# Reading and multiplying the second gate's weights after the output projection instead of beside it

## The chip, the cores and the metric

The kernel runs on one core of a Trainium2 chip. The metric is the time of one execution on the device in microseconds (us); the median of several runs is compared. Times inside a run are counted from the first instruction of the profiled execution.

## What is computed

One decoder layer on 256 tokens of width 2048, all in float32. A conditioning vector `c` gives six vectors of 2048 numbers (shift, scale and gate for each of two sub-layers):

```
mod = SiLU(c) @ W_ada + b_ada            # W_ada is 2048 x 12288: six blocks of 16 MiB
h = x * (1 + scale1) + shift1
y = W_out [ GatedDeltaNet(h) || ForgettingAttention(h) ]
x = LayerNorm(alpha * x + (1 + gate1) * y)
h = x * (1 + scale2) + shift2
y = MoE(h)      # router: best of 4 groups, in it the best 2 of 8 SwiGLU experts
x = LayerNorm(alpha * x + (1 + gate2) * y)
```

The change is about `gate2`, the sixth block of `W_ada`. Nothing needs it before the last residual: it becomes the row `g2` from the tenth pair of experts on.

## The kernel before, in words

**The stages.** The mixer with its input projections runs to about 580 us. The output projection (`w_out`, lines 899 to 944; its matmuls are recorded at L916) runs from 580 to 710 us, the first layer norm and the router (lines 946 to 1045) to 725 us, and 32 experts in 16 pairs from there to 1670 us. Each expert reads three 4 MiB matrices (`wg`, `wu`, `wd`) in tiles of 1 MiB, whatever tokens it gets. All these reads are issued from SP, in one queue.

**The gate as it was.** `ada_full(s)` (L274) is a generator that handles one block of `W_ada`: for each of 16 `j` it asks for a tile `waf` and reads 1 MiB into it (L283). Then either TensorE multiplies it, four matmuls 32 columns wide into the PSUM tile `paf` (L289; float32 matmuls stand twice in the trace), or VectorE adds it, scaled, to a sum `S` (L232, L234; two instructions a tile), as the table `DVEJ` says. At the end the sum `S` is folded into `paf` (L295), copied to `asum` (L297) and turned into a column by small matmuls (`pac`, L300). `ada_step(n)` runs n such steps. In the output projection, 6, 6 and 4 steps stand behind its first three quarters (`WREST`), 8 tiles for TensorE and 8 for VectorE.

**The output projection.** It runs over four quarters `n` of 512 columns. Each quarter reads four tiles `w_out` (L906), splits every 128 rows on ScalarE (`wh`, L373) and VectorE (`wl`, L374), multiplies 6 times for each of 16 `kt` (`pwo`, L916), then applies gate 1 (L933, L934), transposes the result (`put`, L937), and adds its part of the router's logits (`plg`, L942).

**The buffers.** `wtile` gives one of 6 tiles of 1 MiB, the ring W, used by `w_out`, by `waf` and later by experts' weights. `etile` deals the experts' tiles out over the ring E (5 tiles), then W (6), then E2 (1), and again. The three first tiles of expert 0 are pages. So expert 0 takes three pages and the five E tiles; expert 1 takes the six W tiles, E2, and the first E tile again, once expert 0 has used it. PSUM has two tiles of two banks (`bank2`: `pwo`, later `pye` and `pcb`), two single banks `d` (`dbank`), one `a` (`abank`) and one `m`. `ebank` gives `a` at every third request, but only when no block of `W_ada` is left.

**Order.** Each engine works in order. A planner at build time puts each engine's instructions, and SP's reads, into an order by its own cost estimates, following the program's order where several are ready. The matmuls of the experts' part (`pe_matmul`, recorded at L1051) are told to keep the program's order.

**Experts.** `load_gu(e)` (L1079) asks for the eight tiles of `wg` and `wu`, `stage_a` gathers the tokens (`pga`) and multiplies (`pgu`), `load_d` (L1090) asks for the `wd` tiles of both experts of a pair, and `stage_b` multiplies them (`pye`).

Of the kernel before, what the change touches and what calls it, by code (L numbers as in the profile page):

```python
# [6 lines left out]
F32 = mybir.dt.float32  # L7
# [8 lines left out]
S = 256  # L16
# [20 lines left out]
RORD = (3, 4, 2, 5)  # L37
OVP = 8
CEN = (1,)
WREST = (6, 6, 4, 0)  # L40
DVEJ = {3: 10, 4: 10, 2: 10, 5: 8}
DVET = {(0, 0): 0, (0, 1): 0, (4, 0): 2, (4, 1): 2, (8, 0): 5, (8, 1): 5}
CONVP = dict.fromkeys(('q0', 'k0', 'v0', 'q1', 'k1', 'v1'), (1, 2))
CONVN = {'v0': 0, 'v1': 1}
# [4 lines left out]
def build(tc, A, out, dbg=None, stop=None):  # L49
# [15 lines left out]
    with ctx:  # L65
# [9 lines left out]
        turn_ = [0]  # L75

        def page(name, dt=F32):
            return pg.tile([128, 2048], dt, name=name, tag="P")
# [7 lines left out]
        def dbank(name, dt=F32):  # L86
            return pd.tile([128, 512], dt, name=name, tag="d")

        def abank(name):
            return pa.tile([128, 512], F32, name=name, tag="a")  # L90

        def ebank(name):

            turn_[0] += 1
            return abank(name) if turn_[0] % 3 == 0 and not ada_units else dbank(name)

        def bank2(name):
            return pacc.tile([128, 1024], F32, name=name, tag="acc")
# [6 lines left out]
        fp = front.enter_context(tc.tile_pool(name="fp", bufs=2))  # L105
# [167 lines left out]

        def ada_full(s):  # L274

            ps = abank("paf")
            vj = spread(DVEJ[s], 16)
            S_ = None
            if vj:
                S_ = page("S5") if s == RORD[-1] else fp.tile([128, 2048], F32, name="S", bufs=1)  # L280
            for j in range(16):
                w = wtile("waf")
                SP.dma_start(w[:, :2048], wada_v[:, j, s * D:(s + 1) * D])  # L283
                c = cs[:, j:j + 1]
                if j in vj:
                    mac(S_, w[:, :2048], c, 2048, j == vj[0])
                else:
                    for g in range(4):
                        PE.matmul(ps[32 * g:32 * g + 32, :], c.to_broadcast([128, 32]), w[:, g * 512:(g + 1) * 512],  # L289
                                  start=j == 0, stop=j == 15 and not vj)  # L290
                if j < 15:
                    yield
            if vj:
                for g in range(4):
                    PE.matmul(ps[32 * g:32 * g + 32, :], ones[:, 0:32], S_[:, g * 512:(g + 1) * 512], start=False, stop=True)  # L295
            a = wk.tile([128, 512], F32, name="asum", bufs=1)
            V.tensor_copy(a, ps)  # L297
            pc = dbank("pac")
            for i in range(4):
                PE.matmul(pc[:, i * 4:i * 4 + 4], a[:, i * 128:(i + 1) * 128], sel4, start=i == 0, stop=i == 3, skip_group_check=True)  # L300
            dst = gcol[s] if s in gcol else mod2n[:, s - 3]
            V.tensor_tensor(dst.rearrange("p (h i) -> p h i", h=4), pc[:, 0:16].rearrange("p (i h) -> p h i", h=4),
                            bc[:, s].rearrange("p (h i) -> p h i", h=4), op=OP.add)
            if s in (3, 4):
                pp = dbank("pap")
                av = a.rearrange("p (q j) -> p j q", j=16)
                for j in range(16):
                    for h in range(4):
                        PE.matmul(pp[32 * h:32 * h + 32, j * 4:j * 4 + 4], av[:, j, :], sel4, start=j == 0, stop=j == 15, skip_group_check=True)
                for h in range(4):  # L310
                    b = slice(32 * h, 32 * h + 32)
                    V.tensor_tensor(mod2[b, s - 3], pp[b, 0:64].rearrange("p (j h) -> p j h", h=4)[:, :, h], bcp[b, s - 3], op=OP.add)
            yield
# [3 lines left out]
        ada_left = [0]  # L317
# [15 lines left out]
        for dt2 in range(8):  # L333
            ps = dbank("pxt")
# [566 lines left out]
        for n in range(4):  # L901
            ns = slice(n * 512, (n + 1) * 512)
            ws = []
            for q in range(4):
                w = wtile("w_out")
                SP.dma_start(w[:, :2048].rearrange("p (k n) -> p k n", k=4),  # L906
                             w_out[q * 512:(q + 1) * 512, ns].rearrange("(k p) n -> p k n", p=128))
                ws.append(w[:, :2048].rearrange("p (k n) -> p k n", k=4))
            ps = bank2("pwo")

            def terms(kt, part_, wx, first, en):
                for t in range(2):
                    ts = slice(t * 128, (t + 1) * 128)
                    o_ = [oT[kt // 4][:, a, kt % 4, ts] for a in range(2)]
                    for i, h_ in enumerate(o_[:1] if part_ else o_):
                        PE.matmul(ps[:, t * 512:(t + 1) * 512], h_, wx[:, :512], start=first and i == 0, stop=en, skip_group_check=True)  # L916

            g1 = ut[:, 512:1024]
            ACT.activation(g1, bc_row(gcol[2], n, ebank("pg1"), ut[:, 1024:1536]), AF.Copy)
            late = []  # L920
            for kt in range(16):
                wh, wl = split1(ws[kt // 4][:, kt % 4, :], 512)
                terms(kt, 0, wh, kt == 0, False)
                late.append((kt, wl))
                if len(late) > LATE:
                    terms(late[0][0], 1, late[0][1], False, False)
                    late.pop(0)
            for i, (kt, wl) in enumerate(late):
                terms(kt, 1, wl, False, i == len(late) - 1)
            ada_step(WREST[n])  # L930
            for t in range(2):
                pt_ = ps[:, t * 512:(t + 1) * 512]
                V.tensor_tensor(pt_, pt_, g1, op=OP.mult)  # L933
                V.scalar_tensor_tensor(u[t][:, ns], u[t][:, ns], ALPHA, pt_, op0=OP.mult, op1=OP.add)  # L934
                px_ = ebank("put")
                for i in range(4):
                    PE.transpose(px_[:, i * 128:(i + 1) * 128], u[t][:, n * 512 + i * 128:n * 512 + (i + 1) * 128], ident)  # L937
                ui = ut[:, t * 1536:t * 1536 + 512]
                ACT.activation(ui, px_, AF.Copy)
                V.bn_stats(st[:, t, n, :], u[t][:, ns])  # L940
                for i in range(4):
                    PE.matmul(plg[:, t * 36:(t + 1) * 36], ui[:, i * 128:(i + 1) * 128], wr[:, n * 4 + i, :], start=n + t + i == 0,  # L942
                              stop=n * 4 + i == 15, skip_group_check=True)
# [64 lines left out]
        M = sm("M", 2, 4, 8)  # L1008
        V.tensor_tensor(M, og[:, :, :, None].to_broadcast([128, 2, 4, 8]), p12[:, :, None, :].to_broadcast([128, 2, 4, 8]), op=OP.mult)
        Mf = M.rearrange("p t g e -> p (t g e)")  # L1010
        prk = abank("prk")
        PE.matmul(prk[:, 0:64], Us, Mf, start=True, stop=False, skip_group_check=True)
        PE.matmul(prk[:, 32:64], ones, Mf[:, 0:32], start=False, stop=False, skip_group_check=True)
        for t in range(2):
# [237 lines left out]
        def overflow():  # L1252
# [14 lines left out]
            with tc.If(full > CAP):  # L1267
                GP.iota(idx, pattern=[[1, NE]], base=0, channel_multiplier=0, allow_small_or_imprecise_dtypes=True)
                V.memset(ec, 0.0)
                with tc.For_i(0, NE, 1) as e:  # L1270
# [8 lines left out]
                    for b in range(2):  # L1279
# [30 lines left out]
                        for t in range(2):  # L1310
                            for n in range(4):
                                combine_q(t, n, ye, woT, pb[n % 2])

        sp_, xg = slots_of(0)
        weighted(0, sp_)
        how = None
        pieces = []
        for p in range(NE // 2):
            more = p + 1 < NE // 2
            if p:  # L1320
                fill = {j: [f] for j, f in zip(CJ, pieces)}
            else:
                fill = {4 * q: [lambda q=q: gathered(q, sp_, xg)] for q in range(4)}
            gu0 = stage_a(load_gu(2 * p), xg, 0, fill)
            if not p:
                how = weights_of(0, sp_)
            hid = []
            fill = {TJ: [lambda: hid.append(hidden(gu0, 0, sp_))]}
            if ROWS <= p < ROWS + len(ROW):
                for n in range(4):  # L1330
                    fill.setdefault(RJ[n], []).append(lambda n=n: row_part(p - ROWS, n))
            if not more:
                xr = residual()
            w1 = load_gu(2 * p + 1)
            wd = []
            if p == OVP:
                wd = load_d(p, range(2))
                overflow()
            gu1 = stage_a(w1, xg, 1, fill)
            if more:  # L1340
                nsp, nxg = slots_of(p + 1)
                weighted(p + 1, nsp)
                for q in range(2):
                    gathered(q, nsp, nxg)
            hid.append(hidden(gu1, 1, sp_))
            if not more:
                gated(xr)
            else:
                for q in range(2, 4):
                    gathered(q, nsp, nxg)  # L1350
                nhow = weights_of(p + 1, nsp)
                wd += load_d(p, range(len(wd), 4))
                pieces = combine(p, stage_b(wd, hid), how)
                sp_, xg, how = nsp, nxg, nhow
# [63 lines left out]
```

## Time and profile before

| | us |
|---|---|
| median of 3 runs | 1711.81 (1706.97 to 1716.03) |
| profiled execution, its own time | 1716.68 |
| its span, first to last instruction | 1714.9 |
| PE (matmul) busy | 1612.3 (94%) |
| DVE busy | 795.8 (46%) |
| ACT busy | 390.5 (23%) |
| read from memory | 583.77 MB |

How to read it: a busy TensorE is not one at its peak, since its matmuls are pipelined and overlap in the records. The profile also gives the share of time in which the 16 DMA engines moved data, and how fast; this has to be read stage by stage.

### The profile page before, as it was taken

The numbers are of one execution on the slowest core, as the hardware profiler recorded it, in microseconds if no ns is written. First come the engines' busy times: TensorE is split into PE (matmuls) and PEld (weight loads), VectorE is DVE, ScalarE is ACT, GpSimd is POOL, SyncE is SP. The second block draws the span as 40 slices with busy tenths as digits, with TensorE's granted clock in tenths as the row PEclk, the third lists the DMA queues.
The fourth block names the chain that finished last, engine by engine and source line by source line (L and its number), as shares of the span: only waits on it lengthen the run. The fifth ranks groups of instructions, "written<-read, shape, count | busy, mean of one in ns | idle before, by whom it ended". The sixth has DMA issues, their size and how long they took to land. (4 is left out here: it accounts for less than half of the span.)

```text
span 1714.9 us, 23756 instructions
## 1 busy us (share of the span) xinstructions
PE 1612.3 (94%) x9709; PEld 952.6 (56%) x9709; DVE 795.8 (46%) x1538; ACT 390.5 (23%) x699; POOL 64.8 (4%) x80
## 2 busy tenths in 40 slices
PE   5999899999999999799999999999899999999984
PEld 2777777789778866643444344344444434434431
DVE  3568889768747777522322222132222212213166
ACT  1443355344324533400000000000000010010101
POOL 3000001000000000000000000000000000000001
PEclk8899899999999999899999999999999999999997
DMA  9989877527747879869999999999899999999994
GB/s 289 314 296 340 306 263 272 173 99 259 265 152 285 343 276 344 337 260 403 426 424 425 425 425 424 424 425 425 356 425 424 403 424 384 424 394 402 407 412 151
DMA packets 122193, 587.47 MB, mean 343 GB/s; under 512 B 9600, under 2 KB 11824, under 8 KB 65248
## 3 DMA queue, kind: packets, MB, share of 16 engines
q1 hardware_dynamic: 121328, 585.35, 86.4%
q8 instruction: 78, 1.28, 0.3%
q0 software_dynamic: 752, 0.56, 0.3%
q14 instruction: 35, 0.29, 0.0%
HBM read 583.77 MB, written 2.10 MB: 342 GB/s over the span
## 5 line engine op out<-in xcount | busy, mean ns | idle before, releaser
L1051 PE MATMUL pgu<-wu,xg 128*64 128x512 f32 x1024 | 467.5, 598 | 22.6 <-DMA wu<-in_w_up 20.8
L1051 PE MATMUL pgu<-wg,xg 128*64 128x512 f32 x1024 | 465.0, 597 | 2.0 <-DVE xg L1123 2.0
L1051 PEld LDWEIGHTS pgu<-wg,xg 128*64 128x64 f32 x1024 | 131.2, 136 | 197.3 <-issue 188.0
L1051 PE MATMUL pye<-wd,sp 128*64 128x512 f32 x960 | 215.7, 595 | 0.0
L1123 DVE TENSOR_SCALAR xg<-pga,aff 128x128 f32<-128x128 f32 x256 | 87.5, 405 | 264.4 <-PE pga L1051 264.4
L1051 PEld LDWEIGHTS pgu<-wu,xg 128*64 128x64 f32 x1024 | 129.9, 136 | 105.5 <-issue 59.9
L391 PE MATMUL pi<-hH,wh 128*128 128x256 f32 x640 | 168.1, 294 | 3.0 <-ACT wh L373 1.8
L391 PE MATMUL pi<-hL,wh 128*128 128x256 f32 x640 | 165.8, 290 | 0.0
L1051 PEld LDWEIGHTS pye<-wd,sp 128*64 128x64 f32 x960 | 68.0, 137 | 135.8 <-issue 135.5
L391 PEld LDWEIGHTS pi<-hH,wh 128*128 128x128 f32 x640 | 124.4, 194 | 18.4 <-issue 12.8
L1051 PEld LDWEIGHTS pga<-sp,xn 128*128 128x128 f32 x1024 | 118.7, 194 | 15.8 <-issue 14.6
L1161 ACT ACTIVATE gu<-pgu 128x512 f32<-128x512 f32 x32 | 19.1, 597 | 475.8 <-PE pgu L1051 475.8
L1201 DVE SCALAR_TENSOR_TENSOR yy<-pye,wc,yy 128x1024 fp32r<-128x1024 f32 x30 | 38.4, 1281 | 190.5 <-ACT yy L1200 190.1
L391 PEld LDWEIGHTS pi<-hL,wh 128*128 128x128 f32 x640 | 124.3, 194 | 1.1 <-DVE hL L354 0.2
L1051 PE MATMUL pga<-sp,xn 128*128 128x128 f32 x1024 | 123.4, 279 | 1.1 <-DVE tot L1034 1.1
L1212 DVE TENSOR_TENSOR acc<-pcb,acc 128x1024 f32<-128x1024 f32 x56 | 68.5, 1224 | 117.1 <-PE pcb L1051 117.1
L391 PE MATMUL pi<-hH,wl 128*128 128x256 f32 x640 | 105.4, 290 | 3.1 <-DVE wl L374 3.1
L391 PEld LDWEIGHTS pi<-hH,wl 128*128 128x128 f32 x640 | 89.3, 195 | 5.3 <-DVE wl L374 4.6
L1200 ACT ACTIVATE yy<-pye,wc 128x1024 fp32r<-128x1024 f32 x30 | 33.4, 1115 | 255.6 <-PE pye L1051 255.6
L234 DVE SCALAR_TENSOR_TENSOR S<-waf,cs,S 128x1024 f32<-128x1024 f32 x68 | 90.5, 1343 | 0.0
L916 PE MATMUL pwo<-wh,oT 128*128 128x512 f32 x256 | 73.4, 405 | 0.3 <-ACT wh L373 0.3
L1051 PE MATMUL pcb<-yy,ohT 128*128 128x512 f32 x240 | 71.8, 420 | 1.8 <-DVE acc L1212 1.8
(410 smaller groups left out, 1925.2 us busy)
## 6 DMA issues: line engine op xcount, KB each, us to landing
wu<-in_w_up SPq DMA_DIRECT2D x128, 1024.0 KB, 18.7
wg<-in_w_gate SPq DMA_DIRECT2D x128, 1024.0 KB, 17.4
wd<-in_w_down SPq DMA_DIRECT2D x126, 1024.0 KB, 18.3
waf<-in_w_ada SPq DMA_DIRECT2D x64, 1024.0 KB, 5.1
wah<-in_w_ada SPq DMA_DIRECT2D x32, 1024.0 KB, 7.3
w_out<-in_w_out SPq DMA_DIRECT2D x16, 1024.0 KB, 6.7
w_q<-in_w_in SPq DMA_DIRECT2D x8, 1024.0 KB, 7.0
w_k<-in_w_in SPq DMA_DIRECT2D x8, 1024.0 KB, 5.6
```

What stands on the lines that cost most here:

```text
L234: V.scalar_tensor_tensor(S_[:, hs], w[:, hs], c, S_[:, hs], op0=OP.mult, op1=OP.add)
L391: PE.matmul(ps[:, m * 256:(m + 1) * 256], wx[:, m * 128:(m + 1) * 128], h_, start=first and m % 2 == 0 and i == 0, stop=en, skip_group_che ...
L916: PE.matmul(ps[:, t * 512:(t + 1) * 512], h_, wx[:, :512], start=first and i == 0, stop=en, skip_group_check=True)
L1051: return tc.keep_in_program_order(PE.matmul(*a, **k))
L1123: V.tensor_scalar(xg[:, j * 128:(j + 1) * 128], ps[:, i * 128:(i + 1) * 128], aff[:, 0, j:j + 1], aff[:, 1, j:j + 1], op0=OP.mult, op1=OP.add)
L1161: ACT.activation(gu, ps, AF.Copy)
L1200: ACT.activation(y[:, 0], ps[h], AF.Copy, scale=how[0])
L1201: V.scalar_tensor_tensor(y[:, 1], ps[h], how[0], y[:, 0].bitcast(F32), op0=OP.mult, op1=OP.subtract)
L1212: V.tensor_tensor(acc[t][:, hs], pc, acc[t][:, hs], op=OP.add)
```

## The change

Gate 2 has no VectorE tiles any more (`DVEJ` is 0 for block 5), and all its 16 steps stand in one place: behind the router in the program, after a `load_gu(0)` that has moved ahead of them. Its PSUM tile comes from `bank2`, its page `S5` is gone, `ebank` may give bank `a` between two blocks, and the router's rank matmuls (`prk`) take a `dbank`.

```
-WREST = (6, 6, 4, 0)
-DVEJ = {3: 10, 4: 10, 2: 10, 5: 8}
+DVEJ = {3: 10, 4: 10, 2: 10, 5: 0}
...
-            return abank(name) if turn_[0] % 3 == 0 and not ada_units else dbank(name)
+            return abank(name) if turn_[0] % 3 == 0 and (not ada_units or ada_left[0] == 0) else dbank(name)
...
-            ps = abank("paf")
+            ps = bank2("paf")[:, :512] if s == RORD[-1] else abank("paf")
...
-                S_ = page("S5") if s == RORD[-1] else fp.tile([128, 2048], F32, name="S", bufs=1)
+                S_ = fp.tile([128, 2048], F32, name="S", bufs=1)
...
-            ada_step(WREST[n])
...
-        prk = abank("prk")
+        prk = dbank("prk")
...
+        w00 = load_gu(0)
+        ada_step(16)
         sp_, xg = slots_of(0)
...
-            gu0 = stage_a(load_gu(2 * p), xg, 0, fill)
+            gu0 = stage_a(load_gu(2 * p) if p else w00, xg, 0, fill)
```

## Rows read from the trace of the kernel before

**Rows 1.** The page, part 2: busy tenths and GB/s in 40 slices of 42.9 us.
```profile
PE   5999899999999999799999999999899999999984
...
DMA  9989877527747879869999999999899999999994
GB/s 289 314 296 340 306 263 272 173 99 259 265 152 285 343 276 344 337 260 403 426 424 425 425 425 424 424 425 425 356 425 424 403 424 384 424 394 402 407 412 151
```

**Rows 2.** Windows: length; busy of PE, PEld, DVE, ACT, POOL; clock, DMA, GB/s.
```profile
580.00:709.70 129.70, 125.87 (x622) 94.06 (x614) 86.74 (x132) 51.55 (x97) 7.57 (x6) 0.99 0.89 341
...
709.00:725.00 16.00, 6.68 (x36) 5.53 (x35) 11.91 (x54) 9.01 (x6) 0.00 (x0) 0.68 0.76 317
725.00:739.00 14.00, 12.99 (x65) 7.56 (x66) 5.35 (x20) 0.00 (x0) 0.00 (x0) 0.88 0.00 1
739.00:778.00 39.00, 37.99 (x222) 20.06 (x223) 10.37 (x30) 3.25 (x5) 0.00 (x0) 1.00 0.87 349
778.00:840.00 62.00, 62.00 (x316) 26.64 (x314) 15.10 (x28) 4.19 (x6) 0.00 (x0) 1.00 1.00 413
...
840.00:900.00 60.00, 60.00 (x308) 25.92 (x306) 16.70 (x31) 6.42 (x8) 0.00 (x0) 1.00 1.01 425
...
960.00:1020.00 60.00, 57.57 (x285) 26.10 (x282) 15.04 (x29) 4.19 (x6) 0.00 (x0) 1.00 1.01 424
...
1380.00:1440.00 60.00, 60.00 (x286) 25.29 (x286) 15.02 (x28) 6.37 (x10) 4.16 (x4) 1.00 0.95 396
```

**Rows 3.** Timeline of SP's queue, 680 to 782 us: start, length, what it issued.
```profile
688.78 0.33 SPq L1079 DMA_DIRECT2D wg<-in_w_gate  x1
...
707.24 0.33 SPq L1079 DMA_DIRECT2D wu<-in_w_up  x1
...
738.93 0.33 SPq L1079 DMA_DIRECT2D wu<-in_w_up  x1
745.05 15.18 SPq L1090 DMA_DIRECT2D wd<-in_w_down  x8
762.84 0.33 SPq L1079 DMA_DIRECT2D wg<-in_w_gate  x1
...
777.90 0.33 SPq L1079 DMA_DIRECT2D wg<-in_w_gate  x1
```

**Rows 4.** Waits of SP's queue, 560 to 800 us: total, times, longest.
```profile
SPq L1079 <- DVE wl L374: 22.2, 4, 6.8
SPq L1079 <- PE pye L1051: 17.8, 4, 10.8
```

**Rows 5.** Timeline of TensorE, 580 to 685 us: gate 2's work between the quarters.
```profile
616.82 2.78 PE L289 MATMUL paf<-waf,cs 128*32 128x512 f32 x24
...
648.91 2.78 PE L289 MATMUL paf<-waf,cs 128*32 128x512 f32 x24
...
679.10 1.92 PE L289 MATMUL paf<-waf,cs 128*32 128x512 f32 x16
680.84 1.04 PE L295 MATMUL paf<-S,U 128*32 128x512 f32 x8
...
682.70 1.05 PE L300 MATMUL pac<-sel,asum 128*128 128x4 f32 x8 [0.38 <-DVE asum L297]
```

**Rows 6.** Groups by line, 580 to 710 us: busy and mean ns, then idle before.
```profile
L234 DVE SCALAR_TENSOR_TENSOR S<-waf,cs,S 128x1024 f32<-128x1024 f32 x14 | 17.6, 1278 | 0.0
```

**Rows 7.** Timeline of all engines, from the last `pwo` to the first experts.
```profile
708.58 1.10 PE L916 MATMUL pwo<-wl,oT 128*128 128x512 f32 x4
...
722.04 0.66 PE L1012 MATMUL prk<-M,Us 128*128 128x64 f32 x2 [5.29 <-DVE M L1009]
...
724.99 3.60 PE L1051 MATMUL pga<-sp,xn 128*128 128x128 f32 x16 [1.06 <-DVE tot L1034]
...
732.67 2.05 PE L1051 MATMUL pga<-sp,xn 128*128 128x128 f32 x16
```

**Rows 8.** Tile `waf`, the whole run: from issue to landing.
```profile
DMA to landing us min/median/max: 4.7/5.1/12.9
```

**Rows 9.** Tile `wd`, 740 to 830 us: its first use by TensorE.
```profile
L1051 PE MATMUL pye<-wd,sp x66: 592/592/643, 774.2 to 829.6; 128*64 128x512 f32 x66
```

## The prediction, made before the changed kernel ran

> **What bounds the kernel now.** I read the slices first [rows 1]. Up to slice 17 the reads run well below their later rate while TensorE is busy; from slice 18 (771 us) on they stand at 424 to 426 GB/s with few exceptions. So the kernel has a front bound by TensorE and an experts' part bound for most of its length by reads. The table by windows says it more sharply [rows 2]: from 840 us the DMA engines are full at 425 GB/s, and in 960 to 1020 TensorE lacks 2.4 us of 60. In the part that makes rows for the last layer norm, about 1293 to 1588 us, TensorE is full again (1380 to 1440: 60 of 60, reads 396 GB/s); but that part starts when the reads before it are done, so a shift of the reads is passed on to the end.
>
> The experts' time therefore hangs on one number: when the stream of experts' tiles, running full, would have had to start. A 1 MiB tile at 425 GB/s takes 1.0486 / 0.425 = 2.47 us. From 739 to 840 us the core read 349 x 39 + 413 x 62 = 39.2 MB [rows 2], which is 92.2 us at 425 GB/s: the stream acts as if it had started, full, at 747.8 us, with 15 expert tiles already there. Those 15 are expert 0's eight and seven of expert 1's, which fill every buffer before 725 us. Then there is nothing to read into: 1 GB/s from 725 to 739 [rows 2], until expert 0 gives its first E tile back at 738.93 [rows 3].
>
> Why 747.8 and not 739? The queue stops once more, up to 777.90, for a buffer that TensorE frees in the down projection [rows 3, 4], which begins at 774.2 [rows 9]. By then 13 more tiles are issued. So the start of the stream is set in two ways, and the later counts: by how many tiles are still to be read, or by TensorE's pace through the first pair.
>
> **What the change removes.** From the output projection go TensorE's gate work, 2.78 + 2.78 + 1.92 + 1.04 + 1.05 = 9.6 us [rows 5], and VectorE's: 14 instructions of 1.28 us, 17.6 us, and the two that begin the sum [rows 6]. TensorE is busy 125.87 of the stage's 129.70 us [rows 2], so its part counts nearly whole; VectorE's 86.74 lie beside it and count nothing, except at the ends of quarters, where TensorE waits for it within the 3.8 us that it is idle. The last `pwo` moves forward by 7.5 us (only the L289 work, with no gain from the rest) to 13.4 us (everything and the idle too). I take 9, near the sum, because I see nothing else that fills TensorE less: 709.7 becomes 700.7 us.
>
> Also gone from this stage are 16 tiles of reads, 39.5 us of a full queue. That is the price: the stage ran at 341 GB/s [rows 2] and now has less to read, since only the six W tiles can take gate tiles in advance.
>
> **What it adds.** Sixteen reads and 64 matmuls (128 records) on TensorE, 16 x 0.93 = 14.8 us at the rate of the blocks of 24 [rows 5], up to 16 x 1.05 = 16.8 if each stands alone (the same 8 records of another 32-column form took 1.04), and the small matmuls again. From 709.0 to 725.0 TensorE was busy 6.68 of 16 us [rows 2], so 9.3 us of it find room there; about 6.7 us come on top.
>
> **The sum by reads.** The four W tiles of the last quarter came free one by one, from 688.78 to 707.24 us, by VectorE's split [rows 3, 4]; 9 us earlier they take gate tiles. With the two of the third quarter, five gate tiles are read and the sixth is on its way when the last `pwo` ends. Left at 700.7 are then about 11 gate tiles and seven of expert 1: 18 x 2.47 = 44.4, to 745.1 us. Against 747.8 that is **2.7 us earlier**.
>
> **The sum by TensorE.** The first down projection, 774.2, moves by -9 + 6.7 = -2.3, and so does the buffer of 777.90: **2.3 us earlier**. The later of the two counts, 2.3 us. Both give nearly the same because what is taken out of one stage is put into the next; the gap in the reads is filled, and nearly as much reading is lost before it.
>
> **The rest of the edits.** `load_gu(0)` moves ahead of the gate, past no other read but those, and uses pages and E tiles that no gate tile uses: nothing; were it late, each tile would cost 2.47 us. SP issues 16 reads of some 0.33 us each as before; queued behind them stand expert 1's six W tiles and all later experts, which is why the sum counts all of them. POOL issues none of the moved reads. `paf` in a two-bank tile must be copied before the second `pye` tile is needed, some 770 us; it is done by about 735, and if not, each microsecond later costs one. `prk` and `ebank` change banks: between 0.7 us lost (the wait of one copy) and as much gained at each quarter; I take nothing.
>
> **A rule weighed.** The clock shows 0.68 in 709 to 725 and 0.88 in 725 to 739 [rows 2], between its two levels of 1.2 and 2.4 GHz; the first gather's 16 records took 3.60 us, the second's 2.05 [rows 7]. Before that, TensorE had waited 5.29 us for the router [rows 7]. I take the full clock for the gate, since it fills just those waits. At the lower level everywhere the 6.7 us on top would be some 13, and the first pair 4 us later than now: +4 in place of -2.3. The Trainium skill, TensorE: Matmul & The Clock Gate, in the section on why this matters, warns of the very loop that this change makes, a wait for a read before each short burst of matmuls, which it says leaves TensorE at the low clock. By that rule the sum would be the +4. The trace has no such loop to show, only the fall in the router's waits.
>
> **The rivals.**
>
> *The gap is filled for nothing.* From 709 to 739 the queue moved 317 x 16 + 1 x 14 = 5.1 MB of 12.75 [rows 2]: 18 us unused. If the planner lets TensorE take gate tiles in the last quarters, so that W tiles turn over before 700 us, more than six are read there. Four more make the reads 10 us shorter, and a stage shorter by 13 instead of 9 gives the same to TensorE: 9 us faster, at the very most 18. For it: the queue is not full there (341 GB/s). Against it: TensorE is, so what it does early it does at the cost of `pwo`. The Trainium skill, Perfetto Trace Analysis, Optimization Strategy, says that interleaving stages with different limits may pay; by it the result is here. Median 1703 or less.
>
> *TensorE holds the tiles.* TensorE works in order. If the gate's first matmuls stand behind the rank matmuls, which wait for the router's last step (722.04, now about 713) [rows 7], the six W tiles are full and the queue stops from about 703 to 714. Then 10 gate and six expert tiles remain, 39.5 us and a landing of 4.7 at the least [rows 8] of which 2.5 is in it: 756 us, **8 us later** than 747.8, 1720. If they stand behind the gather as well, 3 us more. It decides from about 4 us of such holding on. This is also the case in which the change does not do what it says.
>
> *The gather waits for the last gate tile.* If all 16 tiles are multiplied ahead of the first gather, that starts when the sixteenth has landed, about 700.7 + 11 x 2.47 + 2.5 = 730 us, where it now starts at 724.99 [rows 7]. Less 1.5 us for a warm gather, the first pair is 3 to 4 us later: 1715.
>
> **How the numbers follow.** The profiled execution took 1716.68 us, 4.9 above the median of the runs; by its own time the forecast is 1714.4, by the median 1711.81 - 2.3 = 1709.5. I give the forecast 0.38, the filled gap 0.25, the held tiles 0.20, the waiting gather (and the low clock, which ends in the same place) 0.17. A measurement of this kernel can tell about 0.5% from no change, 8.6 us, so 1703.2 to 1720.4 counts as the same. Faster by more is the filled gap and a little of the forecast: 0.27. Slower by more is rather more than half of the held tiles and a few of the rest: 0.16. The rest, 0.57, is the same. The range, 1698 to 1723, takes in the held tiles, behind the gather too, and most of the filled gap.
>
> **What would show it.** Right: the last `pwo` near 701; no window of 1 GB/s around 730; reads at full rate from some 700 us on; expert 1's W tiles landing after the gate's, to about 745; the first `pye` near 772. Wrong: the queue idle between 703 and 714 (held tiles), a first gather at 728 or later behind a wait for `waf`, or more than six gate tiles issued before the last `pwo` (filled gap). If the reads do not run full behind the gap, or a shift of the stream is not passed on to the end, the reasoning itself is wrong.

## The result, and the profile after

The changed kernel took 1727.35 us, median of five runs (1721.75 to 1731.91), beside 1710.19 for the kernel before, also of five. The ratio on record is 1.0086, with a 95% interval of 1.0058 to 1.0114; it is an estimate of its own and not the quotient of the two medians, which is 1.0100. By the ratio the change is **slower by some 15 us**; 1709.5 was forecast, with 1723 as the upper end of the range.

The profiled execution of the changed kernel, 1721.75 us, is the fastest of its five. Its span of 1720.0 us is only 5.1 longer than that of before, but it reached the first `pwo` at 573.34 us, where the kernel before did at 580.41, although both issue the same instructions up to there. So I count from the first `pwo` on. From there to the end of the span it is 1134.5 us before and 1146.7 after: **12.2 us lost**. Line numbers after are one or two lower.

The page's slices, beside [rows 1]:

```profile
PE   5999899999999999699999999999899999999984
...
DMA  9889877538647874989999999999899999999994
GB/s 288 310 292 353 313 262 255 172 108 294 241 168 288 325 269 152 413 321 405 425 423 426 424 425 424 425 425 424 368 424 425 401 425 384 423 395 401 404 412 151
```

The slice with little reading has moved: 152 GB/s in slice 15 (645 to 688 us, 344 before), 413 in slice 16 (337 before). From slice 18 on the two rows are alike. So the change plays before 775 us, and the rest is passed on.

TensorE, from the last `pwo` on (start, length, what, and in brackets the wait before), beside [rows 5, 7]:

```profile
686.77 1.09 PE L915 MATMUL pwo<-wl,oT 128*128 128x512 f32 x4
687.79 1.90 PE L288 MATMUL paf<-waf,cs 128*32 128x512 f32 x10
...
697.93 1.06 PE L288 MATMUL paf<-waf,cs 128*32 128x512 f32 x8 [0.21 <-DMA waf<-in_w_ada]
700.68 0.43 PE L1010 MATMUL prk<-M,Us 128*128 128x64 f32 x2 [1.69 <-DVE M L1007]
...
701.69 1.06 PE L288 MATMUL paf<-waf,cs 128*32 128x512 f32 x8
710.37 1.93 PE L288 MATMUL paf<-waf,cs 128*32 128x512 f32 x8 [7.61 <-DMA waf<-in_w_ada]
712.85 1.94 PE L288 MATMUL paf<-waf,cs 128*32 128x512 f32 x8 [0.55 <-DMA waf<-in_w_ada]
...
727.77 1.06 PE L288 MATMUL paf<-waf,cs 128*32 128x512 f32 x8 [0.65 <-DMA waf<-in_w_ada]
729.65 1.30 PE L299 MATMUL pac<-sel,asum 128*128 128x4 f32 x8 [0.81 <-DVE asum L296]
730.80 3.42 PE L1049 MATMUL pga<-sp,xn 128*128 128x128 f32 x16
```

Read it from the top. The output projection ends 113.4 us after its first `pwo` (128.2 before). Eight gate tiles (of 8 records each) are done by 702.8, seven of them ahead of the rank matmuls and the eighth right behind; they hardly delay these: `prk` comes 13.9 us after the last `pwo`, 13.5 before. Then TensorE stands for 7.61 us, and the other eight come one every 2.49 us, the time of a 1 MiB read. Only behind the last of them, and the small `pac`, is the first gather, `pga`, at 730.80: 157.5 us after the first `pwo`, 144.6 before. The gather's input `sp` had been written by VectorE 25 us earlier:

```profile
704.67 0.42 DVE L1104 TENSOR_TENSOR sp<-slots,slot 128x256 f32<-128x256 f32 x1
705.12 0.42 DVE L1109 TENSOR_TENSOR sp<-sp,W 128x256 f32<-128x256 f32 x1
```

What SP issued in that time (start, length, what):

```profile
653.82 31.94 SPq L282 DMA_DIRECT2D waf<-in_w_ada  x6
687.89 0.33 SPq L1077 DMA_DIRECT2D wg<-in_w_gate  x1
688.92 2.73 SPq L282 DMA_DIRECT2D waf<-in_w_ada  x2
691.70 0.46 SPq L1077 DMA_DIRECT2D wg<-in_w_gate  x1
692.21 0.47 SPq L1077 DMA_DIRECT2D wu<-in_w_up  x1
692.73 0.64 SPq L1077 DMA_DIRECT2D wg<-in_w_gate  x1
693.47 21.70 SPq L282 DMA_DIRECT2D waf<-in_w_ada  x8
...
728.90 15.99 SPq L1077 DMA_DIRECT2D wu<-in_w_up  x2
750.68 15.17 SPq L1088 DMA_DIRECT2D wd<-in_w_down  x8
...
783.53 0.33 SPq L1077 DMA_DIRECT2D wg<-in_w_gate  x1
```

Before the stage's end six gate tiles are issued, one for each W tile. Then come ten more, with **four tiles of expert 0 among them** (687.89 and 691.70 to 692.73). Expert 1's W tiles follow, and at 728.90 the queue stops for a buffer that TensorE frees only at 744.56, because the experts' products begin so late; and again up to 783.53, 210.2 us after the first `pwo` (777.90 before [rows 3], 197.5).

The waits of SP's queue, 640 to 800 us (total, times, longest), beside [rows 4]:

```profile
SPq L282 <- DVE wl L373: 34.7, 6, 7.9
SPq L1077 <- PE pgu L1049: 23.1, 4, 15.3
SPq L1077 <- PE pye L1049: 18.6, 4, 10.8
```

The gate's reads wait for VectorE's split of `w_out`, which frees the W tiles, and the experts' reads for the products of the first pair.

### The profile page after: what moved, and what is told of

The parts are those of the page before. It is cut to its first block, busy times and chain, and to the rows that moved or that the text cites. A ratio compares the mean times of both kernels' runs of the same rounds, so it can differ in the third digit from the quotient of the medians.

```text
span 1720.0 us, 23850 instructions
## 1 busy us (share of the span) xinstructions
PE 1615.2 (94%) x9765; PEld 944.3 (55%) x9765; DVE 776.4 (45%) x1522; ACT 390.6 (23%) x699; POOL 64.2 (4%) x80
## 5 line engine op out<-in xcount | busy, mean ns | idle before, releaser
L1049 PEld LDWEIGHTS pga<-sp,xn 128*128 128x128 f32 x1024 | 118.6, 194 | 17.2 <-issue 17.2
L233 DVE SCALAR_TENSOR_TENSOR S<-waf,cs,S 128x1024 f32<-128x1024 f32 x54 | 72.9, 1357 | 0.0
```

The costliest lines, as they stand in the source:

```text
L233: V.scalar_tensor_tensor(S_[:, hs], w[:, hs], c, S_[:, hs], op0=OP.mult, op1=OP.add)
L1049: return tc.keep_in_program_order(PE.matmul(*a, **k))
```

## The experiments

Up to the first `pwo` all kernels issue the same work, but their profiled executions reached it between 573.3 and 585.7 us. That spread drops out if times are counted from there. For each kernel the table has the median and the ratio on record to the kernel before in the same comparison, and from its profile, in us after the first `pwo`: the last `pwo` (the start of its last group of four), the first `pga`, the first `pye`, and the end of the span. **Unused** is the read time that the queue let pass in the first 300 us, from four windows: their length times (1 - GB/s / 425), summed. For the kernel before, 120 us at 338, 30 at 276, 50 at 282 and 100 at 423 GB/s give 24.6 + 10.5 + 16.8 + 0.5 = 52.4; for the changed one 51.7 + 0.3 + 10.6 + 2.1 = 64.7.

Windows of the kernel before (length; busy of PE, PEld, DVE, ACT, POOL; clock, DMA, GB/s):

```profile
580.41:700.41 120.00, 116.20 (x580) 86.93 (x577) 83.20 (x126) 49.06 (x94) 7.57 (x6) 0.99 0.89 338
700.41:730.41 30.00, 20.17 (x94) 16.35 (x94) 18.98 (x74) 11.49 (x10) 0.00 (x0) 0.77 0.67 276
730.41:780.41 50.00, 48.49 (x278) 24.58 (x276) 12.12 (x35) 3.25 (x5) 0.00 (x0) 1.00 0.71 282
780.41:880.41 100.00, 100.00 (x500) 42.28 (x497) 25.03 (x41) 8.00 (x11) 0.00 (x0) 1.00 1.01 423
```

The same windows of the changed kernel:

```profile
573.34:693.34 120.00, 119.12 (x577) 92.27 (x574) 72.59 (x127) 52.90 (x98) 7.06 (x6) 1.00 0.67 242
693.34:723.34 30.00, 16.63 (x102) 4.26 (x106) 8.78 (x51) 8.44 (x5) 0.00 (x0) 0.72 1.01 421
723.34:773.34 50.00, 45.97 (x243) 21.27 (x236) 8.27 (x23) 2.86 (x4) 0.00 (x0) 0.93 0.84 335
773.34:873.34 100.00, 100.00 (x511) 44.36 (x511) 30.12 (x56) 7.79 (x11) 0.00 (x0) 1.00 1.00 416
```

| kernel | median | ratio, interval | last `pwo` | `pga` | `pye` | end | unused |
|---|---|---|---|---|---|---|---|
| before | 1710 to 1715 | | 128.2 | 144.6 | 193.8 | 1134.5 | 52.4 |
| changed | 1727.35 | 1.0086, 1.0058 to 1.0114 | 113.4 | 157.5 | 206.5 | 1146.7 | 64.7 |
| freed_gather | 1719.56 | 1.0034, 1.0022 to 1.0046 | 113.8 | 136.7 | 195.8 | 1138.7 | 57.4 |
| gate_reads_first | 1728.24 | 1.0069, 1.0049 to 1.0089 | 113.4 | 132.2 | 195.2 | 1144.9 | 63.2 |
| reads_only | 1699.27 | 0.9928, 0.9901 to 0.9954 | 113.6 | 132.0 | 181.4 | 1121.7 | 39.5 |
| no_gate | 1703.39 | 0.9934, 0.9917 to 0.9951 | 113.6 | 132.0 | 182.0 | 1121.5 | 79.2 |
| vector_part | 1719.75 | 1.0036, 1.0022 to 1.0050 | 113.5 | 132.4 | 190.3 | 1137.5 | 55.2 |
| six_in_gap | 1720.93 | 1.0043, 1.0027 to 1.0060 | 113.4 | 132.3 | 195.2 | 1137.2 | 55.4 |
| expert_tiles_last | 1721.94 | 1.0059, 1.0040 to 1.0079 | 114.2 | 151.7 | 201.7 | 1141.3 | 59.5 |
| vector_in_stage | 1726.81 | 1.0061, 1.0040 to 1.0082 | 139.7 | 156.2 | 206.1 | 1145.5 | 64.4 |
| ten_in_stage | 1709.95 | 0.9971, 0.9953 to 0.9989 | 118.6 | 139.2 | 188.6 | 1130.2 | 47.1 |
| eight_in_stage | 1702.45 | 0.9919, 0.9904 to 0.9935 | 117.4 | 135.8 | 185.2 | 1125.6 | 43.7 |
| old_bank_turn | 1725.08 | 1.0057, 1.0038 to 1.0076 | 113.4 | 157.6 | 206.9 | 1147.4 | 65.2 |
| tensor_in_stage | 1716.79 | 1.0011, 0.9995 to 1.0027 | 130.6 | 147.0 | 196.2 | 1134.8 | 54.3 |

Compare the last two columns. Against the kernel before, "unused" and "end" move together to within 2 us in every row, though the edits are very different (no_gate also reads 16 tiles less, 39.5 us: 79.2 - 39.5 = 39.7). So the time can be counted as the read time that goes unused in the first 300 us. This is bookkeeping and not yet a cause; what follows asks what leaves it unused.

**freed_gather.** The gate's tiles from the seventh on stand between expert 0's steps:

```diff
+GA = 6
+GJ = range(3, 13)
...
+                        if s == RORD[-1]:
+                            tc.keep_in_program_order(k_)
...
-        ada_step(16)
+        ada_step(GA)
...
+                for j in GJ:
+                    fill.setdefault(j, []).append(lambda: ada_step(1))
```

> Of the changed kernel's gate, six tiles are multiplied ahead of the first gather and the other ten one by one between the steps of expert 0's gate and up product, in a fixed order; the same 16 reads and 64 matmuls. Theory 1 (in the changed kernel the first gather is held behind the sixteenth gate tile): the gather comes about 133 us after the first pwo, where the changed kernel has 157.5 and the kernel before 144.6; the stream's last stop (for expert 1's first free buffer) 10 to 15 us earlier than the 210 us after the first pwo of the changed kernel; 1711 to 1717 us, about the kernel before. Theory 2 (16 reads moved out of the output projection delay the stream of reads, whatever the order on TensorE): the reads are the same, so no gain, 1724 to 1730. Theory 3 (TensorE's 15 us of gate work, part of it at the low clock): the work is still in the way of the first pair, 1722 to 1728.

Measured: `pga` at 136.7, and 1719.56, 8 us below the changed kernel, by the ends after the first `pwo` too. The hold is real and costs about that much, with the same reads and the same matmuls. But setting the gather free does not bring the kernel back to before, as theory 1 had it, and the time lies between the ranges of theories 1 and 3: from `prk` on TensorE works with hardly a break (67 of the 68.6 us to `pye`), and its gate work lies in the open.

```profile
705.76 0.69 PE L1014 MATMUL prk<-M,Us 128*128 128x64 f32 x2 [5.34 <-DVE M L1011]
...
707.61 7.75 PE L290 MATMUL paf<-waf,cs 128*32 128x512 f32 x48
...
715.29 2.05 PE L1053 MATMUL pga<-sp,xn 128*128 128x128 f32 x16
...
774.38 1.08 PE L1053 MATMUL pye<-wd,sp 128*64 128x512 f32 x4
```

From `prk` to `pye` it is 68.6 us here; before, 722.04 [rows 7] to 774.2 [rows 9], 52.2. The 16.4 us on top are all 16 tiles, 14.9 us at 0.93, and the small matmuls.

**gate_reads_first.** The call stands one statement further down:

```diff
         w00 = load_gu(0)
-        ada_step(16)
...
                 how = weights_of(0, sp_)
+                ada_step(16)
```

> As the changed kernel, but the gate's step stands one statement further down, which puts ten gate reads ahead of the four last tiles of expert 0 instead of among them; TensorE's order is unchanged. Theory 1, with the four tiles read among the gate's as a part of the price: the sixteenth gate tile lands up to 10 us earlier and the gather starts about 147 us after the first pwo instead of 157.5; but the first expert products then wait for expert 0's tiles, so little of it stays: 0 to 6 us faster than the changed kernel, 1721 to 1727. Theory 2: the sum of reads is the same, 1727. Theory 3: 1727.

The expectation was wrong about the kernel itself. The reads kept their order: four tiles of expert 0 still go out among the gate's (SP issues them at 695.25 and 699.05 to 700.45, the last eight gate tiles from 700.68 on). What moved is TensorE's work: the planner put the last eight gate tiles behind the first gather, which came at 132.2. The run tells more for that. `pye` came at 195.2, as early as in freed_gather, and yet the kernel ended 6.2 us later. The waits of SP's queue from 694 us on say why:

```profile
SPq L282 <- PE paf L288: 29.4, 8, 14.7
```

Gate tiles sit in the W tiles until TensorE, busy with expert 0, comes to them, and the queue stands behind them: 259 and 170 GB/s in the ten microseconds from 140 and from 150 us after the first `pwo`, where the changed kernel had 420 and 423. A gate tile that waits holds up either the gather or the queue.

**reads_only.** Nothing multiplies gate 2's tiles, and gate 2 is its bias alone:

```diff
+                if s == RORD[-1]:
+                    pass
...
+            if s == RORD[-1]:
+                V.tensor_copy(gcol[5], bc[:, 5])
...
```

> The 16 reads of gate 2 stay where the changed kernel has them, but nothing multiplies them: gate 2 is its bias alone. Theory 1: nothing holds the gather, which comes about 131 us after the first pwo (144.6 before); the reads, 39.5 us of a full queue, fit into the gap of before: 1698 to 1708. Theory 2: the reads themselves are the price: 1720 to 1728, as the changed kernel. Theory 3: as theory 1, since TensorE's gate work is gone: 1698 to 1708; freed_gather tells it from theory 1.

**no_gate.** Nothing reads them either:

```diff
-        ada_step(16)
+        V.tensor_copy(gcol[5], bc[:, 5])
```

> Gate 2 is neither read nor multiplied: it is its bias alone. It prices the whole of what was moved. Theory 1: the gather about 131 us after the first pwo, and with no gate tile in the way of the experts' reads the stream waits for TensorE alone: 1692 to 1702, 10 to 18 us below the kernel before. Theory 2: the same, and far from reads_only, by 15 us or more. Theory 3: the same, and near reads_only.

1699.27 and 1703.39 (the second 1.4 us above its range), with equal ends after the first `pwo` (1121.7 and 1121.5): the 16 reads by themselves cost nothing. Theory 2 falls. In reads_only 13 of the 16 are issued by 681.4 us, ahead of the last `pwo` at 687.0, because no W tile has to wait for a multiplication; that stage reads at 302 GB/s, not 242. What the gate costs is that its tiles occupy buffers and TensorE until they are multiplied.

**vector_part.** Six tiles on TensorE in the router's wait, ten on VectorE between expert 0's steps (placed as in freed_gather; TensorE adds VectorE's sum in expert 1's product):

```diff
+VJ5 = range(GA, 16)
...
-            vj = spread(DVEJ[s], 16)
+            vj = spread(DVEJ[s], 16) if s != RORD[-1] else VJ5
...
```

> The changed kernel, with the gate's first six tiles on TensorE as there (in the router's wait) and the other ten on VectorE, between expert 0's steps; TensorE adds VectorE's sum in one block in expert 1's product. The reads are the same 16 in the same places. Theory A (the time is TensorE's load and its waits from the first pwo to the first pye; reads of the gate cost nothing as long as something frees their tiles): only about 2 us of TensorE work is left over reads_only, whose first pye came 181.4 us after the first pwo: 182 to 187 here, 1700 to 1706. Theory B (VectorE, at 2.5 us a tile as slow as the reads, takes over the hold: the gather's evictions queue behind tiles that have not landed): first pye at 190 to 200, 1708 to 1720.

The gather is not held (132.4), but `pye` came at 190.3 and the time was 1719.75. This is theory B's range, and in part its reason: TensorE waited 6.5 us for the gathered tokens `xg`, which VectorE copies out of PSUM (0.5 in freed_gather). The larger part is in the first of the four windows: every kernel that multiplies no gate tile inside the output projection, reads_only apart, leaves 50.3 to 51.7 us unused in its first 120 us (242 to 247 GB/s). The kernel before has 52.4 in all. So by this count, and as long as nothing frees W tiles inside the stage, **no order of the work behind it can win more than some 2 us**. The 14 kernels bear this out; it is not shown for orders that were not tried.

**six_in_gap.** As freed_gather, with the first six tiles free to run in the router's wait (edit against freed_gather):

```diff
-                        if s == RORD[-1]:
+                        if s == RORD[-1] and j >= GA:
                             tc.keep_in_program_order(k_)
```

> As freed_gather, but the first six gate tiles are free to run in the router's wait, ahead of the rank matmuls, as in the changed kernel; the other ten stay between expert 0's steps. Theory A: six tiles at 0.93 us leave TensorE's path: 5.6 us below freed_gather's 1719.6, so 1712 to 1716, first pye 190 us after the first pwo (195.8 there). Theory B (the order of the gate's work on TensorE matters only by holding the gather, and the reads set the rest): as freed_gather, 1718 to 1722.

The gather moved 4.4 us forward, the end after the first `pwo` only 1.5, and the medians (1719.56, 1720.93) show no gain: theory B. The gather's first 16 records took 3.75 us, where freed_gather's, right behind 48 gate matmuls, took 2.05; and 55.4 us unused is near the floor just named.

**expert_tiles_last.** TensorE's order as in the changed kernel, for which the last gate tiles are told to keep the program's order; of expert 0's four late tiles three are read behind the gate's:

```diff
+                        if s == RORD[-1] and j > 10:
+                            tc.keep_in_program_order(k_)
...
+        ada_step(16)
         w00 = load_gu(0)
-        ada_step(16)
```

> TensorE's order exactly as in the changed kernel, with the gather behind all 16 gate tiles; only the reads change: three tiles of expert 0 that are read among the gate's there come behind them here. Theory A: the sixteenth tile lands 3 x 2.5 = 7.4 us earlier and the gather starts about 150 us after the first pwo (157.5 there), but the products then wait for some of the three tiles; 2 to 6 us below the changed kernel: 1721 to 1725. Theory B (the sum of reads counts, not their order): 1726 to 1729.

The gather came at 151.7, 5.8 us earlier, the end 5.4 us earlier, 1721.94: theory A. The tiles read among the gate's are a term of their own. That rests on the profiles, since the intervals of the two ratios overlap (1.0040 to 1.0079 and 1.0058 to 1.0114). The last gate tile's matmuls began even 8.0 us earlier, 7.4 of them the reads of three tiles, but the way from there to the gather took 5.31 us at a granted clock of 0.50, where the changed kernel had 3.03 at 0.92:

```profile
723.41 1.94 PE L288 MATMUL paf<-waf,cs 128*32 128x512 f32 x8 [0.55 <-DMA waf<-in_w_ada]
726.16 1.87 PE L301 MATMUL pac<-sel,asum 128*128 128x4 f32 x8 [0.81 <-DVE asum L298]
```

**vector_in_stage** and **tensor_in_stage** change only the gate's split, in the kernel before (the 16 of the table gives VectorE 15 tiles, since tile 0 stays on TensorE):

```diff
-DVEJ = {3: 10, 4: 10, 2: 10, 5: 8}
+DVEJ = {3: 10, 4: 10, 2: 10, 5: 16}
```

> The kernel before, with 15 instead of 8 of gate 2's tiles multiplied on VectorE; everything stays in the output projection. Theory A (TensorE alone bounds that stage): seven tiles at 0.93 us, 6.5 us, leave TensorE; VectorE goes from 87 to some 102 of 130 us: 5 to 7 us below the kernel before, 1706 to 1710. Theory B (VectorE's split of w_out comes late, and TensorE waits for it): no gain or a loss, 1713 to 1722.

```diff
-DVEJ = {3: 10, 4: 10, 2: 10, 5: 8}
+DVEJ = {3: 10, 4: 10, 2: 10, 5: 0}
```

> The kernel before with all 16 tiles of gate 2 on TensorE in the output projection, none on VectorE. Theory A (VectorE's share cost the stage nothing; TensorE's 0.93 us a tile counts alone): last pwo 134 to 135 us after the first (128.2 before), less some 1 us for the sums: 1718 to 1721. Theory B (VectorE's share cost the 14.8 - 9.6 = 5 us that TensorE's does not account for): 129 to 130 us after the first, 1713 to 1716.

Seven more tiles on VectorE make the stage 11.5 us longer, not 6.5 shorter, and at 1726.81 the time is above the range of theory B as well (1713 to 1722). TensorE waits 5.6 us for `wh`, the converted `w_out`, and 5.0 for `u` from VectorE (0.3 and 2.4 before). The waits explain only a part. The first 120 us read, beside the same window of the kernel before:

```profile
582.97:702.97 120.00, 106.57 (x471) 81.01 (x468) 93.17 (x134) 43.83 (x85) 7.56 (x6) 0.90 0.83 310
```

In the whole stage, 582.97 to 723.70 us, TensorE is idle for 13.4 us, 9.6 more than before [rows 2]. It is also busy for longer, 127.3 us against 125.9, though 6.5 us of gate work went, for the granted clock is 0.92 there and not 0.99. By an estimate from these busy times (127.3 - 125.9 + 6.5) the lower clock cost some 8 us. It had fallen after the waits, to 0.61 from 623 to 633 us and to 0.50 from 663 to 673.

With all 16 on TensorE the stage is only 2.4 us longer, though eight tiles, 7.4 us, came on and the sums, 1.04 [rows 5], went: VectorE's eight had cost 7.4 - 1.0 - 2.4 = 4.0 us in the stage, as theory B nearly had it. Of these, 1.9 us are less idle time (1.9 us, 3.8 before) and some 1.3 the clock (1.00, 0.99 of 130 us before). In both runs VectorE is no free engine there, even at 87 busy us of 130 [rows 2].

**old_bank_turn.** The edit of `ebank` undone:

```diff
-... and (not ada_units or ada_left[0] == 0) else dbank(name)
+... and not ada_units else dbank(name)
```

> The changed kernel with the one edit undone that lets the transposes of the output projection use a third PSUM bank. Theory A (the gate's work alone shortened the stage by 14.8 us): last pwo 113.4 us after the first, as there; 1724 to 1730. Theory B (the third bank carries a part of the 14.8): 115 to 118 us, and the rest of the kernel that much later, 1727 to 1733.

Last `pwo` at 113.4 again, and the same time within its interval: theory A, the bank does nothing.

**ten_in_stage** and **eight_in_stage** take the kernel before and move only as many gate tiles as may find room. Of the tiles that stay in the stage every second one remains on VectorE (`VJ5`), so its share falls from eight to five and to four; `prk` is in another bank, as in the change. The second edit is shown against the first:

```diff
-WREST = (6, 6, 4, 0)
+WREST = (4, 4, 2, 0)
+VJ5 = (1, 3, 5, 7, 9)
...
-        prk = abank("prk")
+        prk = dbank("prk")
...
+        w00 = load_gu(0)
+        ada_step(16 - sum(WREST))
         sp_, xg = slots_of(0)
...
```

> The kernel before, with ten of gate 2's tiles left in the output projection (four, four and two behind its first quarters, five of them on VectorE) and six moved behind it, as many as there are W tiles, to be multiplied on TensorE in the router's wait; no tile is left for the time behind the rank matmuls. Theory A (the price of the change is the tiles beyond the sixth, which land one by one while the gather stands behind them, and the read time that the stage leaves unused): six sixteenths of the stage's 14.8 us go, 5.5, and the router's wait hides the six tiles: first pye about 188 us after the first pwo (193.8 before), 1706 to 1710. Theory B (any gate tile behind the stage delays the rank matmuls or the gather by its landing): 1713 to 1720.

```diff
-WREST = (4, 4, 2, 0)
-VJ5 = (1, 3, 5, 7, 9)
+WREST = (4, 4, 0, 0)
+VJ5 = (1, 3, 5, 7)
...
-        w00 = load_gu(0)
         ada_step(16 - sum(WREST))
+        w00 = load_gu(0)
```

> As ten_in_stage with eight and eight, the eight read ahead of the rest of expert 0's tiles. The seventh and eighth need a W tile that TensorE gives back after the stage's end. Theory A: if they land within the 13 us between the last pwo and the rank matmuls, 14.8 x 8/16 = 7.4 us go: first pye at 186, 1704 to 1708; if not, the rank matmuls stand behind them and 2 to 5 us are lost again: 1707 to 1713. Theory B: 1714 to 1722.

1709.95 (ratio 0.9971) and **1702.45 (ratio 0.9919, interval 0.9904 to 0.9935): faster than both kernels**. Theory A, `pye` at 188.6 and 185.2, as expected to 1 us; the second time lies some 1.5 us below its range. How much of the gain is VectorE's smaller share and how much TensorE's, these two runs do not separate. TensorE in eight_in_stage:

```profile
696.18 1.09 PE L917 MATMUL pwo<-wl,oT 128*128 128x512 f32 x4
697.21 1.90 PE L290 MATMUL paf<-waf,cs 128*32 128x512 f32 x10
...
708.27 1.44 PE L296 MATMUL paf<-S,U 128*32 128x512 f32 x7
710.20 0.41 PE L1013 MATMUL prk<-M,Us 128*128 128x64 f32 x2 [0.49 <-DVE M L1010]
...
711.09 1.03 PE L301 MATMUL pac<-sel,asum 128*128 128x4 f32 x8
```

The eight tiles and their sum fill the router's wait to within 0.49 us of its end, and behind `prk` only the small `pac` is left ahead of the gather, which waits for its own input. The stage still reads:

```profile
578.81:698.81 120.00, 119.00 (x580) 91.02 (x576) 77.43 (x125) 51.83 (x97) 7.57 (x6) 1.00 0.81 302
698.81:728.81 30.00, 25.90 (x169) 13.86 (x169) 16.68 (x73) 9.05 (x6) 0.00 (x0) 0.94 1.00 408
```

## Why the prediction was wrong

**What bounds the kernel** was right. In all 13 other kernels "unused" and the end move together to within 2 us, so a shift of the stream reaches the end whole. That its start is the later of two counts fits: here `pye` is 12.7 us later and the end 12.2, while vector_part has its `pye` 3.5 us earlier than before and still ends 3.0 later.

**"I take 9"**, for the stage, was mis-sized: 14.8, beyond the upper bound of 13.4. TensorE's gate work, 9.6, went, and with it most of its idle time (0.9 us is left of 3.8) and the time it ran below full clock (1.3 us, 0.99 of 129.7 [rows 2]); that is 13.8 of the 14.8. The clock was not in the sum, and VectorE's part was at nothing except at the quarters' ends; tensor_in_stage puts that part at 4.0, the clock included. Alone this would have made the kernel faster.

**The sum by reads**, 2.7 us earlier, holds as a floor: the kernels without gate work in the stage have 50.3 to 51.7 us unused after 120 us, 0.7 to 2.1 below the 52.4 of before. It was not the later count.

**The sum by TensorE** is the step that failed, in its overlap: "9.3 us of it find room there; about 6.7 us come on top", from which 2.3 us earlier. Measured, the first `pye` is 12.7 us later (206.5 against 193.8). I weighed the room against TensorE's work and not against the arrival of what it works on. Eight tiles, 7.4 us, found their room; the other eight were not there. They came one per 2.49 us, up to 728.8, in front of a gather whose input was ready about 132 us after the first `pwo`: at 705.5 here, and the gather came at 132.0 in reads_only and no_gate, which is 705.3 here. So it stood 25.5 us: 5.1 until the ninth tile, 17.4 for seven more, 3.0 for the last one's matmuls and `pac`. Less the gather's earlier readiness, 144.6 - 132.0 = 12.6 us, that is 12.9 lost, and nearly all of it is passed on, 12.7 to `pye` and 12.2 to the end.

**"The gather waits for the last gate tile"** was the rival that came true, priced at 3 to 4 us. It had 11 tiles left and nothing between them. There were ten, and four of expert 0 among them: from the last `pwo`, 686.8 + 1.1, 14 x 2.47 = 34.6 and a landing of 4.6 give 727.1, where the last tile's matmuls begin at 727.77.

**"`load_gu(0)` ... nothing; were it late, each tile would cost 2.47 us"**: it was late, four tiles, 9.9 us of reads. Taking three of them out of the way, 7.4 us, gave back 5.4 (expert_tiles_last); the products waited for none of them there, and 2.3 us were lost at the low clock between the last gate tile and the gather.

**The filled gap** did not come: TensorE took no gate tile before 687.79, and the queue was at 242 GB/s in the stage. **The held tiles** did not come here either. gate_reads_first has a hold of that kind, with tiles that wait behind the gather: it is 10.4 us behind the kernel before, where 8 were said, and 3 more behind the gather.

**The rule weighed.** The granted clock was 0.50 in the ten microseconds from 703.34 and 0.67 in the twenty after, while TensorE waited for a tile, multiplied it and waited again:

```profile
703.34:713.34 10.00, 2.42 (x12) 0.40 (x16) 1.96 (x9) 0.00 (x0) 0.00 (x0) 0.50 1.02 425
713.34:733.34 20.00, 14.67 (x76) 4.81 (x69) 0.86 (x2) 0.00 (x0) 0.00 (x0) 0.67 1.02 422
```

That is the lower level, 1.2 GHz, and its mix with 2.4. It cost next to nothing here: a tile at the low clock takes 1.9 us, below the 2.49 at which tiles come, the last tile ran at the full clock again (1.06 us), and the gather took 3.42 us, no more than the 3.60 of before [rows 7]. The Trainium skill, TensorE: Matmul & The Clock Gate, in the section on why this matters, says that a long wait for a read before every matmul lets the clock fall; on the clock the trace agrees. The price came from the waiting itself. Where TensorE sets the pace the lower clock is not free: vector_in_stage lost some 8 us to it, by the estimate above. The rule's +4 was also added up too low: it doubled only the 6.7 us on top, but at 1.9 us a tile all 16 take some 30, which less the room of 9.3 and the 9 that went gives +12 or so. That this is near the 12.7 measured is chance, since TensorE's work did not set the pace.

## What to carry to other kernels

Work moved "into a wait" fits as far as its inputs have arrived by then, not as far as the engine is free. Count the buffers that can take them in advance, and those that come free and are filled again before the wait ends (six and two here), and let everything beyond that number stay where the reads were hidden. Then ask what the planner's order puts behind the last of the moved pieces. Here half of the move (eight tiles of 16) was worth 0.8%, and the whole of it cost 0.9%. Between eight and 16 no number was tried.

## What was not expected of the hardware

The same instructions brought the profiled executions to the first `pwo` at 573.3 to 585.7 us, a spread of 12 us in a front of 580. Most of it goes with the granted clock: the four shortest fronts (573.3 to 575.8) have 0.97 and TensorE busy for 533 us, the six longest (579.8 to 585.7) 0.95 to 0.96 and 539 to 542, for the same matmuls. What lowers the clock was not tried. The spread is as large as what the change costs, so the profiles of two kernels are compared from a common instruction on, not by their spans.

VectorE and ScalarE were at 87 and 52 of 130 us in the output projection, and still eight tiles on VectorE cost that stage 4.0 us, and seven more of them 11.5: 9.6 of waits and some 8 of lower clock, less the 6.5 of work that went.
